# The gate map's one-hot tiles stored token by token, with each slot's values in pairs

## The chip, the cores and the metric

The kernel runs on one core of a Trainium2 chip. The metric is the device time of one execution in microseconds. Engines are named as the profile names them: PE is TensorE (PEld its weight loads), DVE is VectorE, ACT is ScalarE, POOL is GpSimd, SP is the queue of SyncE that issues most transfers.

## The reference

Two transformer blocks over 256 tokens of width 1024. The first is an attention block with a gated feed-forward part. The second has two layers, each a mixing part and then a product-key expert part, `peer`, which is what the change touches:

```python
def peer(h, w_q, sub_keys, u_emb, v_emb):
    ...
    def block(x_t):
        q = jnp.einsum('td,dhk->thk', x_t, w_q).reshape(T, PEER_HEADS, 2, PEER_HALF)
        s = jnp.einsum('thpk,hpnk->thpn', q, sub_keys).astype(jnp.float32)
        sv, si = lax.top_k(s, K)
        cand = (sv[:, :, 0, :, None] + sv[:, :, 1, None, :]).reshape(T, PEER_HEADS, K * K)
        cidx = (si[:, :, 0, :, None] * PEER_NKEYS + si[:, :, 1, None, :]).reshape(T, PEER_HEADS, K * K)
        fv, fpos = lax.top_k(cand, K)
        eidx = jnp.take_along_axis(cidx, fpos, axis=-1)
        gate = jax.nn.softmax(fv, axis=-1)
        u = u_emb[eidx]
        v = v_emb[eidx]
        act = jax.nn.gelu(jnp.einsum('thkd,td->thk', u, x_t).astype(jnp.float32), approximate=False)
        return jnp.einsum('thk,thkd->td', (gate * act).astype(x_t.dtype), v)
```

Every token has 8 heads with 16 experts each, so 128 slots; an expert is a pair (i, j) of two keys, each out of 128, and has a gate.

## The kernel before, in words

The kernel gathers no experts. In each layer it runs over all 16384 of them in two passes. The **first pass** (64 steps, `feat`, lines 298 to 300) computes the activation of every expert for every token. The **second pass** (line 379) sums activation x gate x the expert's row. For the second pass it needs the **gate map** G[i, j, t]: the gate of expert (i, j) for token t, zero where the token didn't choose it.

Float32 accuracy is had from parts. A weight chunk of 128x512 comes from DRAM, ScalarE writes its high part `wh` (line 281), VectorE the low part `wl` as a difference (line 282), and TensorE makes three products of 256 columns for each 128x128 piece (lines 298, 299, 300), so twelve for a chunk and 48 for a step of the first pass. There are five buffers each for `wh` and `wl`.

The gate map is built beside the first pass, as side work in portions. `slots` (lines 1445 to 1447) puts the slots on the partitions: `ijh` holds the two keys of each slot and token, `gth_` and `gtl_` the gate as a high and a low float16 part. `onehots` (lines 1478 to 1480) makes for four tokens, with four DVE operations of 512 float16 elements counting `onelow` (line 1485): `a`, a one at place i of every slot; `e`, a one at place j; `b`, which is `e` times the high gate; and then `e` itself times the low gate. `build` (lines 1491 to 1493) multiplies, for each of the four tokens, `a` with `b` and `a` with `e` on TensorE over the 128 slots, both into one PSUM tile, and ScalarE writes it to G. That is eight products per build, 64 builds in a layer, 128 in the program.

The tiles `a`, `b` and `e` are stored place by place, the four tokens next to each other; one token's 128 values are then four elements apart:

```python
four = [P, P, 4]
return v[:, None, t0:t0 + 4].to_broadcast(four)
nc.vector.tensor_tensor(e, iota4, over(ijh[:, 1], t0), op=OP.is_equal)
nc.tensor.matmul(pg[:, i, :], a[:, :, i], b[:, :, i], start=True, stop=False)
nc.tensor.matmul(pg[:, i, :], a[:, :, i], e[:, :, i], start=False, stop=True)
```

What sets the order: the side work is taken up by costs and a rate (`pace`, `tick`), a portion after each chunk; `onehots` runs two groups ahead of `build`. The program's scheduler then places instructions on each engine, where each engine works strictly in its order. Tiles `a` and `b` share a pool of five buffers with other work; `e` (`ohe`) has three buffers of its own.

Two other products on TensorE read float16 tiles whose 128 values lie next to each other: line 1439, which sorts the slots just ahead of the gate map, and line 266, products for nothing that run where a norm would let TensorE wait (80 at a time).

Of the kernel before, what the change touches and what calls it, by code (L numbers as in the profile page):

```python
# [8 lines left out]
F32 = mybir.dt.float32  # L9
F32R = mybir.dt.float32r  # L10
F16 = mybir.dt.float16
# [3 lines left out]
OP = mybir.AluOpType  # L15
# [4 lines left out]
P = 128  # L20
S = 256
# [12 lines left out]
# the candidate pairs of two descending lists of 16: rows from..to, columns, place of the first  # L34
# [6 lines left out]
# the reciprocal root's first guess, its first step y (C - x y^2) K, and what weighs its second  # L41
# [4 lines left out]
# columns of the per-partition constants, in the order kernel() lays them out  # L46
# [10 lines left out]
NCOL = _n  # L57

# shape-only constants: name -> width of its [128, width] block
# [14 lines left out]
def body(tc, A, out, dbg=None, stop=None):  # L74
# [26 lines left out]
    cols = const.tile([P, NCOL], F32, name="cols")  # L101
    ck = const.tile([P, NCST_KEEP], F32, name="ck")
    nc.scalar.dma_start(ck, A["cst"][:, 0:NCST_KEEP])
    nc.scalar.dma_start(cols, A["cols"])

    def col(name, i=0, n=None):
        a, b = _COL[name]
        return cols[:, a + i:b] if n is None else cols[:, a + i:a + i + n]
# [13 lines left out]
    iota4 = const.tile([P, P, 4], F16, name="iota4")  # L122
    mod = const.tile([P, 2, 48], F32, name="mod")

    def behind(n):
        """what is traced inside gives way to the next n instructions."""
        return tc.high_priority(offset=-n)

    # ------------------------------------------------------------------ helpers
# [11 lines left out]
    def rms_stats(parts, width):  # L141
        """parts: list of [128, width] APs -> [128, len] tile of 1/rms."""
# [10 lines left out]
    def part_sq(ss, src, t, hf, eng):  # L153
        """ss[:, 2t + hf] = the sum of squares of half hf of tile t of src."""
        accum_sq(ss[:, 2 * t + hf:2 * t + hf + 1], src[:, t, hf * 512:(hf + 1) * 512], eng)

    def inv_root(dst, m, v, half, scale):
        """dst = 1/sqrt(m * scale) for scale = 2 ** (-2 half), to float32's accuracy; v: 5 tiles like dst."""
        y, t, p_, h1, h2 = v
        # half the exponent (a division by 2 ** (2 half) is half in it), a step of second order and one of third  # L160
# [14 lines left out]
    def inv_rms(dst, s0, s1, e=D * EPS):  # L175
        """dst [128, 1] = 1/sqrt((s0 + s1 + e) / 1024) (each [128, 1])."""
# [5 lines left out]
    def inv_rms_w(dst, s0, width):  # L182
        """dst [128, 1] = 1/sqrt(s0 / width + EPS)."""
# [5 lines left out]
    def diag(r):  # L189
        """[128, 128] with r [128, 1] on the diagonal: a transpose through it scales its rows."""  # L190
# [4 lines left out]
    def hl_tiles(kc, pl=None, name="hl"):  # L195
        """feature-major operand [128, kc, 256] as exact float32r parts, in pieces of 4 chunks."""
# [13 lines left out]
    def split_psum(hl, k, src, gain=None, bias=None, scale=None):  # L210
        """chunk(s) k of hl from src (PSUM [128, n, 256]); per-partition gain/bias columns."""
# [24 lines left out]
    def to_T(src, kc, hl, gain=None, bias=None, by=None, ks=None):  # L236
        """src(t, k) -> [128 tok, 128] AP; transposed (with rows scaled by the diagonals by[t]), scaled and split into hl."""
# [17 lines left out]
    def follow(i_, name):  # L255
        """the instruction i_ keeps behind the one named, on its own engine."""
        tc.add_manual_dep(i_.ins, name, mybir.DependencyInfo(mybir.DependencyClass.NoSync, mybir.DependencyReason.DATA), reason="order")

    def keep_warm(n):
        """n matrix products for nothing, where a norm lets TensorE wait long enough for its clock to fall."""  # L260
        ps = pmm.tile([P, 512], F32, name="mm")
        name = ada_p["mm"]
        idle = iota4[:, 0:32].rearrange("p j t -> p (j t)")
# [6 lines left out]
    def load_w(dram, off, per, ada=True):  # L270
        """one raw weight tile: [128, per] floats, contiguous by partition."""
# [5 lines left out]
    def split_w(src, n):  # L277
        """float32r parts of src [128, n <= 512]."""
# [16 lines left out]
    def mmT(ps, hl, k, wh, wl, start, stop):  # L295
        """ps [features, 256] += W[k]^T @ chunk k of hl"""
# [5 lines left out]
    # work that runs beside a stream of weights, in portions between its pieces  # L302
# [21 lines left out]
    def feat(hl, dram, off, evac, late=False):  # L324
        """two chunks of 128 features of (h @ W)^T: evac([128, 2, 256]); W as [128 d][2][8 chunks of d][128]."""
# [10 lines left out]
    def proj(hl, kc, dram, off, n, evac, base=0, quiet=0, turn=None):  # L336
        """[256 tok, n <= 512] = hl^T @ W, W at dram[off] as pieces [128, 4 chunks, n]."""
# [9 lines left out]
        for k in order:  # L347
# [3 lines left out]
            while j < m:  # L351
                # the last two chunks tile by tile, so that the first tile's end comes early
# [1420 lines left out]
```

## Time and profile before

| what | value |
|---|---|
| median of three runs | 2292.16 us (2290.6 to 2295.77) |
| the profiled execution: its own time, its span | 2295.77 us, 2295.8 us |
| PE busy | 2259.0 us, 98% |
| DVE busy | 1753.4 us, 76% |
| ACT busy | 1274.5 us, 56% |
| gate map products, lines 1491 and 1492 | 512 each, from 633.3 to 1892.2 us |

The profile is of one execution, the slowest of the three. TensorE's products overlap each other: the duration of one holds its way through the engine, and the distance from one start to the next is what it takes of the engine's time. The stages of the gate map lie at about 633 to 890 us and 1645 to 1892 us.

### The profile page before, as it was taken

To read this page: it belongs to the slowest core of one execution; us is meant where nothing else is said; L and a number is where in the kernel's file an instruction comes from. 1 tells how busy PE (TensorE), PEld (TensorE's weight loads), DVE (VectorE), ACT (ScalarE), POOL (GpSimd) and SP (SyncE) were. 2 spreads that over 40 slices of the span, in tenths; PEclk is the share of its full clock that TensorE was granted. 3 is DMA by queue.
4 is the path that set the end of the run, shared out by engine and by line. 5 is a ranking of instruction groups with operands and counts; after the bars stand their busy time and mean duration, and the time that the engine had idled before them with its cause. 6 is when DMAs were issued, how large, how long until landed. Compare 5 with 4: busy or idle time off the path is not lost.

```text
span 2295.8 us, 40651 instructions
## 1 busy us (share of the span) xinstructions
PE 2259.0 (98%) x15032; PEld 2053.3 (89%) x15032; DVE 1753.4 (76%) x4239; ACT 1274.5 (56%) x2324; POOL 20.6 (1%) x28
## 2 busy tenths in 40 slices
PE   8999999999999999999999999999999999999998
PEld 7889988899999999887778877999999999888886
DVE  7778887798767675688888888896767665777776
ACT  7656555455455555555555565555555555555554
POOL 0000000000000000000000020000000000000000
PEclk9999999999999999999999999999999999999999
DMA  6256786446655555889889533456555557666664
GB/s 249 97 183 249 275 317 236 168 166 234 212 180 175 183 183 185 289 313 322 318 314 325 209 129 134 169 207 222 192 184 174 175 181 248 252 252 237 245 245 145
DMA packets 107161, 503.59 MB, mean 219 GB/s; under 512 B 12369, under 2 KB 13521, under 8 KB 61650
## 3 DMA queue, kind: packets, MB, share of 16 engines
q1 hardware_dynamic: 87954, 465.19, 57.9%
q10 hardware_dynamic: 18720, 33.72, 3.9%
q8 instruction: 117, 1.92, 0.3%
q0 software_dynamic: 288, 2.10, 0.2%
q14 instruction: 82, 0.67, 0.1%
HBM read 464.25 MB, written 36.70 MB: 218 GB/s over the span
## 4 chain that ended last, share of the span: by engine, by line
PE 85%; DVE 7%; DMA 5%; ACT 1%; issue 1%; DVEq 0%; SPq 0%; ACTq 0%
PE acc L379 21%; PE acc L298 14%; PE acc L299 14%; PE acc L300 14%; DMA k<-act 5%; PE acc L287 4%; PE acc L290 3%; PE acc L291 3%; DVE wl L282 3%; PE mm L1491 3%; PE mm L1492 3%; DVE G L436 1%; PE pt L246 1%; PE pt L300 1%; PE pt L299 1%
## 5 line engine op out<-in xcount | busy, mean ns | idle before, releaser
L281 ACT ACTIVATE wh<-w 128x512 fp32r<-128x512 f32 (+1 forms) x1408 | 882.2, 630 | 847.7 <-PE acc L299 383.9
L282 DVE TENSOR_TENSOR wl<-w,wh 128x512 fp32r<-128x512 f32 (+1 forms) x1408 | 954.7, 689 | 283.1 <-ACT wh L281 275.2
L298 PE MATMUL acc<-q,wh 128*128 128x256 f32 x2592 | 745.2, 288 | 0.7 <-ACT q L223 0.7
L299 PE MATMUL acc<-q,wh 128*128 128x256 f32 x2592 | 733.2, 283 | 0.5 <-DVE q L224 0.5
L300 PE MATMUL acc<-q,wl 128*128 128x256 f32 x2592 | 729.8, 283 | 1.2 <-DVE wl L282 1.2
L379 PE MATMUL acc<-wh,q 128*128 128x512 f32 x1984 | 612.1, 390 | 0.0
L298 PEld LDWEIGHTS acc<-q,wh 128*128 128x128 f32 x2592 | 497.9, 192 | 1.5 <-ACT q L223 0.9
L299 PEld LDWEIGHTS acc<-q,wh 128*128 128x128 f32 x2592 | 497.2, 192 | 0.8 <-DVE q L224 0.7
L300 PEld LDWEIGHTS acc<-q,wl 128*128 128x128 f32 x2592 | 495.7, 192 | 1.4 <-DVE wl L282 1.4
L379 PEld LDWEIGHTS acc<-wh,q 128*128 128x128 f32 x1984 | 373.0, 188 | 77.1
L379 PE MATMUL acc<-wl,q 128*128 128x512 f32 x992 | 388.1, 393 | 7.0 <-DVE wl L282 6.7
L379 PEld LDWEIGHTS acc<-wl,q 128*128 128x128 f32 x992 | 186.6, 188 | 52.3 <-DVE wl L282 14.1
L1478 DVE TENSOR_TENSOR ohe<-iota,ijh 128x512 f16<-128x512 f16 x128 | 54.1, 425 | 121.3 <-PE mm L1492 121.3
L1525 DVE SCALAR_TENSOR_TENSOR k<-k,G 128x512 f32<-128x512 f32 x128 | 88.2, 689 | 65.2 <-DMA k<-act 63.8
L1492 PE MATMUL mm<-ohe,k 128*128 128x128 f16 x512 | 128.0, 297 | 0.0
L1491 PE MATMUL mm<-k 128*128 128x128 f16 x512 | 126.6, 293 | 0.0
L1493 ACT ACTIVATE G<-mm 128x512 f32<-128x512 f32 x128 | 76.5, 598 | 38.0 <-PE mm L1492 38.0
L290 PE MATMUL acc<-wl,q 128*128 128x512 f32 (+1 forms) x224 | 89.8, 402 | 0.0
L291 PE MATMUL acc<-wh,q 128*128 128x512 f32 (+1 forms) x224 | 87.1, 397 | 0.0
L1533 DVE TENSOR_TENSOR q<-k,q 128x512 fp32r<-128x512 f32 x126 | 86.2, 684 | 0.7
L287 PE MATMUL acc<-wh,q 128*128 128x512 f32 (+1 forms) x224 | 85.3, 402 | 0.0
L1532 ACT ACTIVATE q<-k 128x512 fp32r<-128x512 f32 x126 | 77.8, 617 | 11.6 <-DVE k L1525 11.4
(458 smaller groups left out, 2316.4 us busy)
## 6 DMA issues: line engine op xcount, KB each, us to landing
w<-in_peer_u_dram SPq DMA_DIRECT2D x128, 1024.0 KB, 5.3
w<-in_peer_v_dram SPq DMA_DIRECT2D x128, 1024.0 KB, 4.9
act<-k ACTq DMA_DIRECT2D x128, 256.0 KB, 4.7
k<-act SPq DMA_DIRECT2D x128, 256.0 KB, 5.3
G<-in_ada_w_dram SPq DMA_DIRECT2D x52, 512.0 KB, 7.3
w<-in_w_gu_dram SPq DMA_DIRECT2D x22, 1024.0 KB, 4.9
adw<-in_ada_w_dram SPq DMA_DIRECT2D x44, 512.0 KB, 5.5
w<-in_peer_w_q_dram SPq DMA_DIRECT2D x16, 1024.0 KB, 4.7
```

Source lines behind the costliest of these rows:

```text
L281: ada_p["act"] = nc.scalar.activation(h[:, :n], src, AF.Copy).ins.name
L282: i_ = nc.vector.tensor_sub(l[:, :n], src, h[:, :n].bitcast(F32))
L287: i_ = nc.tensor.matmul(ps, lh, wh, start=start, stop=False)
L290: nc.tensor.matmul(ps, lh, wl, start=False, stop=False)
L291: i_ = nc.tensor.matmul(ps, ll, wh, start=False, stop=stop)
L298: nc.tensor.matmul(ps, wh, h, start=start, stop=False)
L299: nc.tensor.matmul(ps, wh, l, start=False, stop=False)
L300: nc.tensor.matmul(ps, wl, h, start=False, stop=stop)
L379: nc.tensor.matmul(ps[t, hf], lhs, ww[hf], start=first and lhs is h and ww is wh, stop=last and lhs is l)
L1491: nc.tensor.matmul(pg[:, i, :], a[:, :, i], b[:, :, i], start=True, stop=False)
L1492: nc.tensor.matmul(pg[:, i, :], a[:, :, i], e[:, :, i], start=False, stop=True)
L1525: nc.vector.scalar_tensor_tensor(wt, ag, 1.0 / GATE, G[0][:, 2 * n:2 * n + 2, :], op0=OP.mult, op1=OP.mult)
```

## The change

One token's 128 places now lie in a row, in the order [4 tokens, 128 places]. VectorE must then read one slot's value for 128 places in a row, so every value is stored twice (`ijg`, with a last dimension of 2), and the patterns go by pairs: 4 tokens, 64 times, 2. The four arrays of `slots` become one tile. The iota is no longer written four times over. `e` has two buffers in place of three. Apart from that the per-partition constants `cols` are loaded in two transfers (those of the first block into a pool that is given up later). Comments are dropped, so line numbers move by up to 14.

```diff
-    iota4 = const.tile([P, P, 4], F16, name="iota4")
+    iota = const.tile([P, P], F16, name="iota")
...
-    nc.scalar.dma_start(cols, A["cols"])
+    nc.scalar.dma_start(cols, A["cols"][:, NCOL_1:NCOL])
...
+    cols_1 = xp.tile([P, NCOL_1], F32, name="cols_1")
+    nc.scalar.dma_start(cols_1, A["cols"][:, 0:NCOL_1])
...
-        ijh = ip.tile([P, 2, S], F16, name="ijh")
-        gth_ = ip.tile([P, S], F16, name="gth_")
-        gtl_ = ip.tile([P, S], F16, name="gtl_")
+        ijg = ip.tile([P, 4, S, 2], F16, name="ijg")
...
-            nc.vector.tensor_copy(ijh[:, :, ts_], pt[:, 0:2, :])
-            nc.vector.tensor_copy(gth_[:, ts_], pt[:, 2, :])
-            nc.vector.tensor_sub(gtl_[:, ts_], pt[:, 2, :], gth_[:, ts_])
+            nc.vector.tensor_copy(ijg[:, 0:2, ts_, :], pt[:, 0:2, :].unsqueeze(3).to_broadcast([P, 2, P, 2]))
+            gt = pt[:, 2, :].unsqueeze(2).to_broadcast([P, P, 2])
+            nc.vector.tensor_copy(ijg[:, 2, ts_, :], gt)
+            nc.vector.tensor_sub(ijg[:, 3, ts_, :], gt, ijg[:, 2, ts_, :])
...
-        four = [P, P, 4]
+        four = [P, 4, P // 2, 2]
-        def over(v, t0):
-            return v[:, None, t0:t0 + 4].to_broadcast(four)
+        def over(w, t0):
+            return ijg[:, w, t0:t0 + 4, None, :].to_broadcast(four)
+        def pairs_of(v):
+            return v.rearrange("p t (j a) -> p t j a", a=2)
+        places2 = iota.rearrange("p (j a) -> p j a", a=2)[:, None].to_broadcast(four)
         def onehots(t0):
-            ab = st.tile([P, 2, P, 4], F16, name="k2", bufs=NK2)
+            ab = st.tile([P, 2, 4, P], F16, name="k2", bufs=NK2)
             a, b = ab[:, 0], ab[:, 1]
-            e = ip.tile(four, F16, name="ohe", bufs=3)
-            nc.vector.tensor_tensor(e, iota4, over(ijh[:, 1], t0), op=OP.is_equal)
-            nc.vector.tensor_tensor(a, iota4, over(ijh[:, 0], t0), op=OP.is_equal)
-            nc.vector.tensor_mul(b, e, over(gth_, t0))
+            e = ip.tile([P, 4, P], F16, name="ohe", bufs=2)
+            nc.vector.tensor_tensor(pairs_of(e), places2, over(1, t0), op=OP.is_equal)
+            nc.vector.tensor_tensor(pairs_of(a), places2, over(0, t0), op=OP.is_equal)
+            nc.vector.tensor_mul(pairs_of(b), pairs_of(e), over(2, t0))
...
-            nc.vector.tensor_mul(e, e, over(gtl_, t0))
+            nc.vector.tensor_mul(pairs_of(e), pairs_of(e), over(3, t0))
...
-                nc.tensor.matmul(pg[:, i, :], a[:, :, i], b[:, :, i], start=True, stop=False)
-                nc.tensor.matmul(pg[:, i, :], a[:, :, i], e[:, :, i], start=False, stop=True)
+                nc.tensor.matmul(pg[:, i, :], a[:, i, :], b[:, i, :], start=True, stop=False)
+                nc.tensor.matmul(pg[:, i, :], a[:, i, :], e[:, i, :], start=False, stop=True)
```

The order of instructions moves at two places. The first is VectorE at the head of the first layer's gate map. The numbers tell the tiles apart: `ohe_7902`, `ohe_7946`, `ohe_7984` and `ohe_8039` belong to the first four groups of tokens, `wl_8126` is the low part of a weight chunk. Before:

```order
L1479 TENSOR_TENSOR k2_8038<-iota4_85,ijh_5446 128x512
L1478 TENSOR_TENSOR ohe_8039<-iota4_85,ijh_5446 128x512
L1479 TENSOR_TENSOR k2_8102<-iota4_85,ijh_5446 128x512
L282 TENSOR_TENSOR wl_8126<-w_8122,wh_8125 128x512
L1480 TENSOR_TENSOR k2_8038<-ohe_8039,gth__5447 128x512
L1485 TENSOR_TENSOR ohe_8039<-ohe_8039,gtl__5448 128x512
L282 TENSOR_TENSOR wl_8142<-w_8122,wh_8141 128x512
L1478 TENSOR_TENSOR ohe_8103<-iota4_85,ijh_5446 128x512
```

With the change, at the same place (between the same two splits `wl`):

```order
L1493 TENSOR_TENSOR k2_8038<-iota_85,ijg_5448 128x512
L1492 TENSOR_TENSOR ohe_7984<-iota_85,ijg_5448 128x512
L1493 TENSOR_TENSOR k2_8102<-iota_85,ijg_5448 128x512
L287 TENSOR_TENSOR wl_8126<-w_8122,wh_8125 128x512
L1494 TENSOR_TENSOR k2_7983<-ohe_7984,ijg_5448 128x512
L1499 TENSOR_TENSOR ohe_7984<-ohe_7984,ijg_5448 128x512
L287 TENSOR_TENSOR wl_8142<-w_8122,wh_8141 128x512
L1492 TENSOR_TENSOR ohe_8039<-iota_85,ijg_5448 128x512
```

The one-hot that must wait for a free buffer stands where it stood, but it is the third group's where it was the fourth's: with two buffers the third group is the first to take over a used one, with three it was the fourth. Both take it over from the first group, so both wait for the same build. The two operations behind `wl_8126` move to the third group with it. TensorE's order in the gate map is unchanged.

The second place is ScalarE at the very start, where `q` are the evictions of the transposed input (they need `cols`) and `wh` the high parts of the first weights. Before:

```order
L103 DMA ck<-in_cst_dram 128x128
L104 DMA cols<-in_cols_dram 128x176
L134 ACT_TABLE_LOAD
L134 ACTIVATE k_205,ssx<-x 128x512
L134 ACTIVATE k_219,ssx<-x 128x512
L223 ACTIVATE q_106<-pt,cols 128x256 x3
L281 ACTIVATE wh<-w 128x420 x3
```

With the change:

```order
L105 DMA ck<-in_cst_dram 128x128
L106 DMA cols<-in_cols_dram 128x133
L424 DMA cols_94<-in_cols_dram 128x43
L139 ACT_TABLE_LOAD
L139 ACTIVATE k_207,ssx<-x 128x512
L139 ACTIVATE k_221,ssx<-x 128x512
L286 ACTIVATE wh<-w 128x420 x3
L228 ACTIVATE q_108<-pt,cols_94 128x256 x2
```

The constants come in two transfers, the first block's second, and the three splits now stand ahead of the evictions.

## Rows read from the trace of the kernel before

**Rows 1.** The page's busy time of each engine: us, share of the span, instructions.

```profile
PE 2259.0 (98%) x15032; PEld 2053.3 (89%) x15032; DVE 1753.4 (76%) x4239; ACT 1274.5 (56%) x2324; POOL 20.6 (1%) x28
```

**Rows 2.** The page's chain that ended last, by engine and by line.

```profile
PE 85%; DVE 7%; DMA 5%; ACT 1%; issue 1%; DVEq 0%; SPq 0%; ACTq 0%
PE acc L379 21%; PE acc L298 14%; PE acc L299 14%; PE acc L300 14%; DMA k<-act 5%; PE acc L287 4%; PE acc L290 3%; PE acc L291 3%; DVE wl L282 3%; PE mm L1491 3%; PE mm L1492 3%; DVE G L436 1%; PE pt L246 1%; PE pt L300 1%; PE pt L299 1%
```

**Rows 3.** Windows in both gate-map stages: length; busy us by engine; clock, DMA share, GB/s.

```profile
640.00:880.00 240.00, 240.00 (x2012) 237.26 (x2011) 167.31 (x356) 130.97 (x220) 0.00 (x0) 1.00 0.54 177
1660.00:1900.00 240.00, 240.00 (x2011) 237.33 (x2010) 162.91 (x343) 130.64 (x219) 0.00 (x0) 1.00 0.54 179
```

**Rows 4.** The page's costliest groups, gate-map products: busy us, mean ns, idle before.

```profile
L1492 PE MATMUL mm<-ohe,k 128*128 128x128 f16 x512 | 128.0, 297 | 0.0
L1491 PE MATMUL mm<-k 128*128 128x128 f16 x512 | 126.6, 293 | 0.0
```

**Rows 5.** Timeline of PE around one build: start us, duration us, engine, line, operation.

```profile
705.31 0.28 PE L300 MATMUL acc<-q,wl 128*128 128x256 f32 x1
705.43 0.28 PE L1491 MATMUL mm<-k 128*128 128x128 f16 x1
705.54 0.30 PE L1492 MATMUL mm<-ohe,k 128*128 128x128 f16 x1
...
706.25 0.29 PE L1492 MATMUL mm<-ohe,k 128*128 128x128 f16 x1
706.50 0.28 PE L299 MATMUL acc<-q,wh 128*128 128x256 f32 x1
```

**Rows 6.** Timeline of PE, contiguous float16 products: the warming ones, then line 1439.

```profile
365.42 4.64 PE L266 MATMUL mm<-iota 128*128 128x128 f16 x80
...
602.84 0.28 PE L300 MATMUL acc<-q,wl 128*128 128x256 f32 x1
602.96 0.62 PE L1439 MATMUL mm<-ident_h,tm 128*128 128x128 f16 x8
603.39 0.37 PE L298 MATMUL acc<-q,wh 128*128 128x256 f32 x1
603.60 0.28 PE L299 MATMUL acc<-q,wh 128*128 128x256 f32 x1
```

**Rows 7.** Single lines: ns min/median/max, first and last start.

```profile
L1491 PEld LDWEIGHTS <-k x512: 112/117/120, 633.3 to 1892.0; 128*128 128x128 f16 x171
...
L1439 PEld LDWEIGHTS <-tm x128: 95/98/102, 589.7 to 1616.9; 128*128 128x128 f16 x128
L1439 PE MATMUL mm<-ident_h,tm x128: 218/219/230, 589.8 to 1616.9; 128*128 128x128 f16 x128
```

**Rows 8.** Groups on DVE, 640 to 880 us: busy us, mean ns, idle before, releaser.

```profile
L282 DVE TENSOR_TENSOR wl<-w,wh 128x512 fp32r<-128x512 f32 x130 | 89.4, 688 | 14.1 <-ACT wh L281 14.1
L1485 DVE TENSOR_TENSOR ohe<-ohe,gtl__5448 128x512 f16<-128x512 f16 x57 | 24.1, 423 | 1.4
L1478 DVE TENSOR_TENSOR ohe<-iota,ijh 128x512 f16<-128x512 f16 x56 | 23.8, 425 | 56.4 <-PE mm L1492 56.4
L1479 DVE TENSOR_TENSOR k<-iota,ijh 128x512 f16<-128x512 f16 x57 | 23.8, 418 | 0.1
L1480 DVE TENSOR_TENSOR k<-ohe,gth__5447 128x512 f16<-128x512 f16 x56 | 23.4, 418 | 0.0
```

**Rows 9.** The largest cast of `slots`: ns min/median/max, first and last start.

```profile
L1445 DVE CAST ijh<-mm x4: 417/421/425, 604.2 to 1617.2; 128x256 f16<-128x256 f32 x4
```

**Rows 10.** Timeline of ACT at the start: transfer of constants, evictions, splits.

```profile
1.19 0.45 ACTq L104 DMA_DIRECT2D cols<-in_cols_dram  x1
...
7.12 0.47 ACT L223 ACTIVATE q<-pt,cols 128x256 fp32r<-128x256 f32 x1 [0.24 <-PE pt L244]
...
8.57 1.43 ACT L281 ACTIVATE wh<-w 128x420 fp32r<-128x420 f32 x3
```

**Rows 11.** Timeline of PE at the start: the first products of the first weights.

```profile
9.16 1.07 PE L287 MATMUL acc<-wh,q 128*128 128x420 f32 x2
```

**Rows 12.** Groups of the whole span: a VectorE operation over 1024 float32 elements.

```profile
L436 DVE SCALAR_TENSOR_TENSOR adw<-adw,cact 128x1024 f32<-128x1024 f32 x44 | 53.3, 1219 | 4.3 <-DMA adw<-in_ada_w_dram 2.6 <-ACT cact L430 1.7
```

More of the change, by code (lines that the diff above doesn't have):

```diff
@@ L57 @@
 NCOL = _n
+NCOL_1 = _COL["norm_mix_2"][0]
 _CST = [
@@ L99, in body @@
     pmm = pool("pmm", 2, PSUM)
-    cols = const.tile([P, NCOL], F32, name="cols")
+    cols = const.tile([P, NCOL - NCOL_1], F32, name="cols")
+    first_cols = []
     ck = const.tile([P, NCST_KEEP], F32, name="ck")
     nc.scalar.dma_start(ck, A["cst"][:, 0:NCST_KEEP])
-    nc.scalar.dma_start(cols, A["cols"])
+    nc.scalar.dma_start(cols, A["cols"][:, NCOL_1:NCOL])
     def col(name, i=0, n=None):
         a, b = _COL[name]
-        return cols[:, a + i:b] if n is None else cols[:, a + i:a + i + n]
+        c = first_cols[0] if a < NCOL_1 else cols
+        if a >= NCOL_1:
+            a, b = a - NCOL_1, b - NCOL_1
+        return c[:, a + i:b] if n is None else c[:, a + i:a + i + n]
     def cst(name):
@@ L262, in keep_warm @@
         name = ada_p["mm"]
-        idle = iota4[:, 0:32].rearrange("p j t -> p (j t)")
+        idle = iota
         for _ in range(n):
@@ L417, in body @@
     x = xp.tile([P, 2, D], F32, name="x")
+    cols_1 = xp.tile([P, NCOL_1], F32, name="cols_1")
+    nc.scalar.dma_start(cols_1, A["cols"][:, 0:NCOL_1])
+    first_cols.append(cols_1)
     ada_q.extend((l, n) for l in range(2) for n in range(48))
@@ L602, in body @@
     nc.sync.dma_start(io_[:, 0:P], A["cst"][:, _CO["iota"][0]:_CO["iota"][1]])
-    nc.vector.tensor_copy(iota4, io_[:, 0:P].unsqueeze(2).to_broadcast([P, P, 4]))
+    nc.vector.tensor_copy(iota, io_[:, 0:P])
     tri = cst_tile(ap_, "tri")
```

## The prediction

> **What bounds the kernel now.** I read the page first: busy shares and the chain that ended last, then the stage that the change touches, then single products in it. TensorE is busy in 98% of the span [rows 1], and 85% of the chain lies on it [rows 2]. The two lines of the gate map, L1491 and L1492, hold about 3% of the span each on that chain [rows 2], so they are work that sets the end, not work beside it. Their stage shows why: between 640 and 880 us, and again between 1660 and 1900 us, TensorE is busy for all 240 of 240 us at the full granted clock, VectorE for 167 and 163, ScalarE for 131, and the DMA engines for 0.54 [rows 3]. TensorE waits for nothing there. Whatever leaves its stream in this stage leaves the end, as long as VectorE keeps ahead.
>
> A busy TensorE says nothing on how fast its products are, because they overlap: one product of L1491 lasts 293 ns and one of L1492 297 ns [rows 4], yet they start about 0.12 us apart [rows 5]. So I price by start to start. In rows 5 a build (eight products, four tokens with a high and a low part) begins at 705.43; the second product of the chunk behind it begins at 706.50. That is 1.07 us for eight builds and one 256-column product, and such a product takes 0.12 us of the stream (602.84 to 602.96 in rows 6). Eight strided builds cost 0.95 us, 0.118 us each, with no extra step into the next chunk.
>
> **The change, part by part.** *The operands in one run.* Each product now reads 128 neighbouring float16 values of a token where it read every fourth, on both operands; number and size of the products stay. The trace has such products already. L1439 sorts the slots with 128x128 float16 products from contiguous tiles, in the same stream between the same chunks: eight begin at 602.96 and the second product of the chunk behind them begins at 603.60, so 0.64 us for what takes 1.07 us with strided operands [rows 6]. The products that keep TensorE warm read one contiguous float16 tile: 80 of them last 4.64 us against 0.62 us for the eight, (4.64 - 0.62) / 72 = 0.056 us apiece [rows 6]. Of the 0.64 us, 8 x 0.056 = 0.45 are the products, 0.12 the chunk's own one, and 0.07 a step into the chunk that the strided builds hide.
>
> A build thus saves 1.07 - 0.64 = 0.43 us. There are 256 / 4 = 64 builds in each of two layers, 128 in all, which agrees with 512 products on each of the two lines, four a build [rows 4]: 128 x 0.43 = **55 us**. Bounds: if the step into the chunk vanishes, 8 x (0.118 - 0.056) = 0.50 us a build, 64 us in all; if the weight loads set the pace at their own 98 ns (L1439's, against 117 for L1491 [rows 7]), 8 x (0.118 - 0.098) = 0.16 us, 20 us in all. I take 0.43: L1439 has the same shapes, type and neighbours, and loads a new weight tile for every product too.
>
> [...]
>
> *The one-hots on VectorE.* Four operations of 512 float16 elements per group of four tokens stay four, at 418 to 425 ns [rows 8]. Their patterns change: the slot's value was read as runs of four, and is now read as one pair, 64 times over per token. No row shows runs of two. The near end is 0.42 us, the same operation with runs of four; the far one is 0.69 us, which is what 512 float32 elements of L282 take [rows 8]. I take 0.42: the result is still float16 with neighbours side by side, and the repeated operand was repeated before too. The cover: a group lasts 240 / 56.5 = 4.25 us now and would last 3.82 us, and VectorE is busy for 167 / 56.5 = 2.96 of it, 78% then. 56 of its idle microseconds are waits at L1478 for the build that frees a buffer [rows 8]; these shrink.
>
> *Two one-hot buffers in place of three.* The order shows that the place of L1478 between the splits `wl` does not move; only the group that it makes is one later build away. It waits for the same build as before. The multiplication by the low part, which its build needs, follows after 0.42 + 0.42 + 0.69 + 0.42 + 0.42 = 2.4 us of VectorE's work; two builds and four chunks of 1.44 us later, over 6 us, that build is due. I put it at nought: the work that hides it is those four chunks. With that cover gone, a build would stand for up to the 2.4 us, and VectorE's splits of the next chunk would be late next.
>
> *Paired lists.* The casts in `slots` write twice the elements: the largest takes 421 ns for 256 elements [rows 9], becomes at most 0.69 us for 512, and the two others are half its size. Four times three such steps of at most 0.27 us are 3 us of VectorE's time in all, from 604 us on and again 1000 us later, beside TensorE's stream. I put them at nought; uncovered they would cost those 3 us. The iota is cast once and becomes shorter. Nought.
>
> *The constants in two transfers.* At the start ScalarE issues one transfer more (0.45 us for the present one) and takes three splits `wh`, 1.43 us, ahead of the first evictions `q`, which come first now at 7.12 us [rows 10]. The first product, at 9.16 us, needs both [rows 11]. So it moves by between nothing and the 1.4 us; I take 0.5 us.
>
> **Sum.** 55.0 - 0.5 = 54.5 us off. The profiled execution took 2295.8 us, its span; 2295.8 - 54.5 = 2241.3. It is the slowest of three, 3.6 us above their median of 2292.16, so on the median's scale **2237.7 us**, say 2238. Its own range is 2228 to 2252: the vanished step at one end, at the other four fifths of the gain and the whole price at the start.
>
> **Rivals.**
>
> *Pairs run at one element per cycle.* If the four operations take 0.69 us, VectorE needs 2.96 + 4 x 0.27 = 4.04 us per group, more than TensorE's 3.82. It becomes the bound, and at best 4.25 - 4.04 = 0.21 us x 128 = 27 us are won: 2265 to 2292, middle 2278. For it: no row shows such runs. Against: the runs of four did not slow down.
>
> *Pairs cost so much that VectorE loses time (the other side).* [...] It decides from (4.25 - 2.96) / 4 = 0.32 us more per operation, 0.74 us [rows 8, 12]. Any price beyond that makes the kernel slower than before. Nothing in the trace points to it.
>
> *The step between elements was not what cost.* Then 0.118 us belongs to these products, contiguous or not, and the time is 2292.2 + 0.5 = 2293. Rows 6 speak against it, unless alternating two moving tiles over one weight tile costs something that L1439 doesn't pay. [...]
>
> *Weight loads at 98 ns set the pace:* 20 us won, 2273.
>
> **How the numbers follow.** Forecast 0.80; one element per cycle 0.06; weight loads 0.04; step not the cost 0.05; slower through the pairs 0.05. The predicted time is the forecast's. The range is 2227 to 2262: the forecast's bounds, stretched at the upper end towards the rivals that still win; the four rivals, 0.20, lie beyond it. A measurement of this kernel tells about 0.2%, 4.6 us, from no change. Faster by more: 0.80 + 0.04 + 0.06 = 0.90; the same 0.05; slower 0.05.
>
> **What would show it.** Right: products of the gate map lasting about 219 ns like L1439's [rows 7], starting 0.056 us apart, 0.64 us from a build's first product to the second of the next chunk; TensorE still busy for all of the stage, which is 27 us shorter in each layer; the four operations at 0.42 us; shorter waits of VectorE at the first one-hot; no change elsewhere. Wrong: the four operations near 0.69 us with TensorE waiting for `wl`; or products that still start 0.1 us apart or more.

## The result and the profile after

The changed kernel takes **2235.8 us** (median of four runs, 2233.88 to 2238.66) against 2292.4 us for the kernel before beside it (2290.6 to 2295.77): the ratio is 0.9754, 95% interval 0.974 to 0.9768. That is 56.6 us less. The forecast was 2238, 54.5 us less, with a range of 2227 to 2262. On another chip, where the kernel before took 2297.61 us, the same program took 2242.67 us (0.9762, 0.9745 to 0.9778).

The profiled execution took 2235.14 us, with a span of 2233.4. The page's busy times answer [rows 1]:

```profile
PE 2201.5 (99%) x15032; PEld 1997.3 (89%) x15032; DVE 1754.2 (79%) x4239; ACT 1265.4 (57%) x2324; POOL 21.5 (1%) x28
```

TensorE ran as many instructions as before and was busy for 57.5 us less; VectorE did the same 1754 us of work in a shorter span. The page's chain of work that ended last, by engine and by line, answers [rows 2]:

```profile
PE 86%; DVE 6%; DMA 5%; ACT 1%; issue 1%; SPq 0%; DVEq 0%; ACTq 0%
PE acc L384 23%; PE acc L303 15%; PE acc L304 14%; PE acc L305 14%; DMA k<-act 4%; PE acc L292 4%; PE acc L295 4%; PE acc L296 4%; DVE wl L287 3%; PE mm L1505 1%; PE mm L1506 1%; PE pt L251 1%; DVE G L444 1%; PE pt L305 1%; PE pt L304 1%
```

The gate map's two lines are now L1505 and L1506, 1% each where they had 3% each. The chunk products of the first pass are L303 to L305, the eviction of a build L1507, the one-hots L1492 to L1494 and the multiplication by the low part L1499. The page's costliest groups (busy us, mean ns, idle before) answer [rows 4]:

```profile
L1505 PE MATMUL mm<-k 128*128 128x128 f16 x512 | 72.3, 222 | 0.0
L1506 PE MATMUL mm<-ohe,k 128*128 128x128 f16 x512 | 70.7, 219 | 0.0
```

One line's instructions (ns min/median/max) answer [rows 7]. Load and product have become those of the slot sort, 98 and 219 ns:

```profile
L1505 PEld LDWEIGHTS <-k x512: 96/98/100, 635.3 to 1830.6; 128*128 128x128 f16 x171
L1505 PE MATMUL mm<-k x512: 219/219/230, 635.3 to 1830.7; 128*128 128x128 f16 x171
```

How much a build takes is read from PE's timeline around one of them (start us, duration us), as in [rows 5]:

```profile
706.70 0.28 PE L305 MATMUL acc<-q,wl 128*128 128x256 f32 x1
706.83 0.23 PE L1505 MATMUL mm<-k 128*128 128x128 f16 x1
706.89 0.22 PE L1506 MATMUL mm<-ohe,k 128*128 128x128 f16 x1
...
707.23 0.22 PE L1506 MATMUL mm<-ohe,k 128*128 128x128 f16 x1
707.25 0.36 PE L303 MATMUL acc<-q,wh 128*128 128x256 f32 x1
707.46 0.28 PE L304 MATMUL acc<-q,wh 128*128 128x256 f32 x1
```

From the build's first product, 706.83, to the second one of the chunk behind it, 707.46, it is 0.63 us where it was 1.07. Over all builds that stand alone the median is 0.632 us (122 of 128; before 1.064 over 124). The products start 56 ns apart (before 118). The gate map's products run from 635 to 873 us and from 1593 to 1831; before they ran from 633 to 898 and from 1627 to 1892 (ahead of the prediction they are given as 633 to 890 and 1645 to 1892). Each layer's stage is 27 us shorter.

The windows inside both stages (length; busy us of PE, PEld, DVE, ACT, POOL; clock, DMA share, GB/s) answer [rows 3]:

```profile
640.00:860.00 220.00, 220.00 (x2055) 217.51 (x2054) 170.91 (x363) 129.32 (x223) 0.00 (x0) 1.00 0.59 199
1620.00:1840.00 220.00, 220.00 (x2049) 217.59 (x2047) 166.76 (x351) 129.68 (x224) 0.00 (x0) 1.00 0.60 198
```

TensorE is still busy for all of the stretch at the full granted clock. VectorE's share rose from 70 to 78%, and has room left. Its groups from 640 to 860 us (busy us, mean ns, idle before) answer [rows 8]:

```profile
L287 DVE TENSOR_TENSOR wl<-w,wh 128x512 fp32r<-128x512 f32 x133 | 91.6, 688 | 15.5 <-ACT wh L286 15.3
L1499 DVE TENSOR_TENSOR ohe<-ohe,ijg 128x512 f16<-128x512 f16 x58 | 24.6, 424 | 1.5
L1494 DVE TENSOR_TENSOR k<-ohe,ijg 128x512 f16<-128x512 f16 x58 | 24.3, 419 | 0.0
L1492 DVE TENSOR_TENSOR ohe<-iota,ijg 128x512 f16<-128x512 f16 x57 | 24.3, 426 | 30.5 <-PE mm L1506 30.5
L1493 DVE TENSOR_TENSOR k<-iota,ijg 128x512 f16<-128x512 f16 x57 | 23.0, 420 | 1.2 <-DMA act<-k 1.1
```

The four operations on pairs take 419 to 426 ns, as the runs of four did. The wait for the build that frees a buffer (at L1492) shrank from 56.4 us in 240 to 30.5 in 220.

**Where the 62.4 us between the two profiled executions lie.** I add up by TensorE's marks. From the first chunk product behind the last scores of the keys (the 33rd chunk product of the first pass over the experts) to the first product of the second pass, the trace holds the whole gate map and the same 3040 chunk products before and after. This stretch is called the first pass from here on: 429.7 and 429.8 us became 402.0 and 402.0, so 27.7 + 27.8 = **55.5 us**. The second pass of the first layer fell from 358.6 to 352.4 us, 6.2 us, but it isn't the change's: its length is 359.2 in the repeat of the changed kernel, while the second layer's is 344.3 in both kernels and in the repeat. The stretch between the layers, from the end of that pass to the second layer's first pass, is 2.5 us shorter (205.8 and 203.3 us). There the granted clock of the kernel before is 0.50 in the windows from 1313 to 1316 and from 1412 to 1415 us, and that of the changed kernel 1.00 all through. Over the runs with the same idle products the stretch takes 202.9 to 203.3 us in the six traces whose clock stays at 1.00 in it and 204.3 to 206.3 in the five whose clock falls. Two of those five have the new moving layout, so it doesn't keep the clock from falling; whether it makes that rarer, some 1 to 3 us a run, is open. Ahead of the first pass 2.0 us were lost, 0.6 of them by the first idle products. Of the rest, the windows from 418 us on show a part (columns as above):

```profile
418.00:420.00 2.00, 2.00 (x7) 1.57 (x8) 0.89 (x3) 0.69 (x2) 0.00 (x0) 0.65 0.00 0
420.00:422.00 2.00, 2.00 (x7) 1.41 (x5) 0.63 (x2) 0.09 (x1) 0.00 (x0) 0.50 0.00 0
```

The granted clock falls to 0.50 after 2 us (416 to 418) in which TensorE ran 11 products; the mark behind it is 1.4 us further back than the one before it. In the same windows of the kernel before and of the changed kernel's repeat it stands at 1.00, with 10 to 12 products in each, so this too is not the change's. So the change is worth 55.5 us in the first passes, less what the start costs, and apart from what it may do to the clock between the layers.

### The profile page after: what moved, and what is told of

The parts are those of the page before. It is cut to its first block, busy times and chain, and to the rows that moved or that the text cites. A ratio compares the mean times of both kernels' runs of the same rounds, so it can differ in the third digit from the quotient of the medians.

```text
span 2233.4 us, 40655 instructions
## 1 busy us (share of the span) xinstructions
PE 2201.5 (99%) x15032; PEld 1997.3 (89%) x15032; DVE 1754.2 (79%) x4239; ACT 1265.4 (57%) x2324; POOL 21.5 (1%) x28
## 4 chain that ended last, share of the span: by engine, by line
PE 86%; DVE 6%; DMA 5%; ACT 1%; issue 1%; SPq 0%; DVEq 0%; ACTq 0%
PE acc L384 23%; PE acc L303 15%; PE acc L304 14%; PE acc L305 14%; DMA k<-act 4%; PE acc L292 4%; PE acc L295 4%; PE acc L296 4%; DVE wl L287 3%; PE mm L1505 1%; PE mm L1506 1%; PE pt L251 1%; DVE G L444 1%; PE pt L305 1%; PE pt L304 1%
## 5 line engine op out<-in xcount | busy, mean ns | idle before, releaser
L286 ACT ACTIVATE wh<-w 128x512 fp32r<-128x512 f32 (+1 forms) x1408 | 881.3, 630 | 827.9 <-PE acc L304 335.5
L303 PE MATMUL acc<-q,wh 128*128 128x256 f32 x2592 | 744.7, 288 | 0.7 <-ACT q L228 0.7
L305 PE MATMUL acc<-q,wl 128*128 128x256 f32 x2592 | 730.0, 283 | 0.0
L303 PEld LDWEIGHTS acc<-q,wh 128*128 128x128 f32 x2592 | 495.3, 191 | 1.3 <-ACT q L228 0.9
L305 PEld LDWEIGHTS acc<-q,wl 128*128 128x128 f32 x2592 | 495.1, 191 | 0.0
L1492 DVE TENSOR_TENSOR ohe<-iota,ijg 128x512 f16<-128x512 f16 x128 | 54.2, 425 | 63.7 <-PE mm L1506 63.6
L1507 ACT ACTIVATE G<-mm 128x512 f32<-128x512 f32 x128 | 75.7, 593 | 1.9 <-PE mm L1506 1.9
L1505 PE MATMUL mm<-k 128*128 128x128 f16 x512 | 72.3, 222 | 0.0
L1506 PE MATMUL mm<-ohe,k 128*128 128x128 f16 x512 | 70.7, 219 | 0.0
```

Source lines behind the costliest of these rows:

```text
L286: ada_p["act"] = nc.scalar.activation(h[:, :n], src, AF.Copy).ins.name
L303: nc.tensor.matmul(ps, wh, h, start=start, stop=False)
L305: nc.tensor.matmul(ps, wl, h, start=False, stop=stop)
L1505: nc.tensor.matmul(pg[:, i, :], a[:, i, :], b[:, i, :], start=True, stop=False)
L1506: nc.tensor.matmul(pg[:, i, :], a[:, i, :], e[:, i, :], start=False, stop=True)
```

## The experiments

**The theories.** Of a product's two operands one, the weights, has a load of its own in the trace (LDWEIGHTS on PEld, 15032 of them beside 15032 products), and the other is called the moving operand; a step is the distance in memory from one of an operand's 128 values to the next. T1: the step of the moving operand is what cost 62 ns a product, and a step in the weight load is hidden beside the products. T2: the weight load's step cost it. T3: either of them is enough. The rival to all three is that another part of the change (two buffers, the constants' two transfers) brought some of the gain. The first four runs share one chip, on which the kernel before took 2298.52 us, 6 more than on the first one, so I go by ratios and by the first passes in the traces; the times that were expected of them are on the first chip's scale.

### One operand strided at a time

The changed kernel with the weights' one-hot interleaved by four tokens again:

```diff
+        def by4(v):
+            return v.rearrange("p t j -> p (t j)").rearrange("p (j t) -> p j t", t=4)
...
-            nc.vector.tensor_tensor(pairs_of(a), places2, over(0, t0), op=OP.is_equal)
+            nc.vector.tensor_tensor(pairs_of(by4(a).rearrange("p j t -> p t j")), places2, over(0, t0), op=OP.is_equal)
...
-                nc.tensor.matmul(pg[:, i, :], a[:, i, :], b[:, i, :], start=True, stop=False)
+                nc.tensor.matmul(pg[:, i, :], by4(a)[:, :, i], b[:, i, :], start=True, stop=False)
...
```

> The changed kernel, but the one-hot of the first list (the operand that is loaded as weights) lies as before, four tokens in turn, so that the weight load reads with a step of 8 bytes; both moving operands stay contiguous. T1 (the step of the moving operand costs all of the 62 ns a product, the loads' step is hidden beside the products): products start 0.056 us apart, and the time is that of the changed kernel, 2234 to 2239 us. T2 (the step of the weight load costs it): 0.118 us apart, 2290 to 2295 us. T3 (either step is enough): also 2290 to 2295 us here.

Measured: 2244.76 us, ratio 0.9758 (0.9732 to 0.9784), as far below the kernel before as the changed kernel. PE's timeline around a build:

```profile
705.66 0.25 PE L1508 MATMUL mm<-k 128*128 128x128 f16 x1
705.74 0.22 PE L1509 MATMUL mm<-ohe,k 128*128 128x128 f16 x1
...
706.31 0.28 PE L304 MATMUL acc<-q,wh 128*128 128x256 f32 x1
```

0.65 us where the contiguous weights give 0.63. First passes of 403.3 and 402.8 us, 1 us over the changed kernel's each. The price turned up where I had not looked for one, on VectorE's groups from 640 to 860 us:

```profile
L1496 DVE TENSOR_TENSOR k<-iota,ijg 128x512 f16<-128x512 f16 x57 | 74.1, 1342 | 0.9 <-DMA act<-k 0.9
L1495 DVE TENSOR_TENSOR ohe<-iota,ijg 128x512 f16<-128x512 f16 x59 | 25.5, 432 | 7.1 <-PE mm L1509 7.1
```

Writing the one-hot with a step of 8 bytes takes 1342 ns where its neighbours take 0.42 us. VectorE's operations overlap too: from its start to the next one's, where they follow each other at once, the strided one takes 1.12 us and its neighbours 0.34. It stayed hidden: the wait at the first one-hot fell from 30.5 to 7.1 us, the one for ScalarE at `wl` from 15.3 to 1.1, and TensorE was busy for all of the 220.

The other half, with both moving operands strided and the slots' values for them in runs of four:

```diff
-            nc.vector.tensor_tensor(pairs_of(e), places2, over(1, t0), op=OP.is_equal)
+            nc.vector.tensor_tensor(by4(e), iota4, over4(jgl[:, 0], t0), op=OP.is_equal)
...
-                nc.tensor.matmul(pg[:, i, :], a[:, i, :], b[:, i, :], start=True, stop=False)
+                nc.tensor.matmul(pg[:, i, :], a[:, i, :], by4(b)[:, :, i], start=True, stop=False)
...
```

> The other half: the weights contiguous, the two moving operands with their step of 8 bytes as before. T1: products 0.118 us apart, no gain is left, 2290 to 2295 us. T2: 0.056 us apart, 2234 to 2239 us. T3: 2290 to 2295 us. If both this run and the one with strided weights come out at 2236, only both steps together cost; if both lie between, each has a part.

Measured: 2295.69 us, ratio 0.9987 (0.9975 to 1.0). PE's timeline around a build:

```profile
706.62 0.27 PE L1515 MATMUL mm<-k 128*128 128x128 f16 x1
706.71 0.30 PE L1516 MATMUL mm<-ohe,k 128*128 128x128 f16 x1
...
707.66 0.28 PE L305 MATMUL acc<-q,wh 128*128 128x256 f32 x1
```

1.04 us, against 1.07 with both strided; first passes of 428.9 us, 0.9 under the kernel before's. T1 holds; T2 and T3 are out. Of the 0.432 us that a build gained, the weights' step has 0.014 to 0.018 and the moving operand's the rest.

### A step of two values

```diff
-        four = [P, 4, P // 2, 2]
+        four = [P, 2, P, 2]
...
-                nc.tensor.matmul(pg[:, i, :], a[:, i, :], b[:, i, :], start=True, stop=False)
+                nc.tensor.matmul(pg[:, i, :], pairs_of(a)[:, i // 2, :, i % 2], pairs_of(b)[:, i // 2, :, i % 2], start=True, stop=False)
...
```

> The changed kernel with tokens interleaved in twos: both operands of every product step by 4 bytes, and the slots' values are read in runs of two tokens, not stored in pairs. [...] If the price is a threshold at anything but neighbours, 0.118 us and 2290 to 2295 us. If it grows with the step, in between: about 0.08 us, 512 x 2 x 0.02 = 20 us over the changed kernel, 2256 us.

Measured: 2244.21 us, ratio 0.9759 (0.973 to 0.9789). PE's timeline around a build:

```profile
709.81 0.23 PE L1504 MATMUL mm<-k 128*128 128x128 f16 x1
709.88 0.22 PE L1505 MATMUL mm<-ohe,k 128*128 128x128 f16 x1
...
710.46 0.28 PE L304 MATMUL acc<-q,wh 128*128 128x256 f32 x1
```

0.65 us a build, the products 58 ns apart, first passes of 402.85 us. So a step of 4 bytes costs 2 ns a product, and 8 bytes cost 60. "Anything but neighbours" is out as the rule, and so is a price that grows evenly from the first step on. Also, VectorE needs no stored pairs here: runs of two tokens, read side by side, take 419 to 425 ns as well.

### All of the change but the layout

```diff
-            e = ip.tile(four, F16, name="ohe", bufs=3)
+            e = ip.tile(four, F16, name="ohe", bufs=2)
...
-    nc.scalar.dma_start(cols, A["cols"])
+    nc.scalar.dma_start(cols, A["cols"][:, NCOL_1:NCOL])
...
```

> The kernel before with all of the change but the layout: two one-hot buffers in place of three, and the constants in two transfers. By my sum: two buffers nought, the start 0 to 1.4 us later (0.5 taken, and 1.1 us seen at the first product of the changed kernel): 2292 to 2294 us. The rival, that part of the 56 us is not the layout's: 2289 us or less. If two buffers cost something while builds are long: over 2296 us, with TensorE waiting at the builds.

Measured: 2299.73 us, ratio 1.0 (0.9987 to 1.0013). Builds of 1.064 us as before, first passes of 429.8 and 430.2 us. The wait at the first one-hot is what it was with three buffers:

```profile
L1486 DVE TENSOR_TENSOR ohe<-iota,ijh 128x512 f16<-128x512 f16 x56 | 23.8, 426 | 56.5 <-PE mm L1500 56.5
```

The time is over the 2296 us that would have spoken for a cost of two buffers, but so is the kernel before beside it, at 2298.52. To within 3 us (the interval), none of the gain is here, and none of it is lost here.

### Steps by themselves

The kernel before; each group of 80 idle products becomes eight kinds of ten. Their results are thrown away in both kernels. (The prediction and the expectation call them products that keep TensorE warm; what they do for the granted clock, no run here shows.)

```diff
+        s3 = flat[:, 0:3 * P].rearrange("p (j t) -> p j t", t=3)[:, :, 0]
+        s4 = iota4[:, :, 0]
...
+                yield lambda: nc.tensor.matmul(ps[:, 0:P], s1, s3, start=True, stop=True)
...
+                yield lambda: nc.tensor.matmul(ps[:, 0:P], s4, s1, start=True, stop=True)
...
-                i_ = nc.tensor.matmul(ps[:, 0:P], idle, idle, start=True, stop=True)
+                i_ = make()
```

> The kernel before; only its idle products that keep TensorE warm differ: each group of 80 becomes eight kinds of ten 128x128 float16 products, with the steps of (weights, moving operand) in bytes (2, 2), (2, 4), (2, 6), (2, 8), (2, 16 within each half of the columns), (4, 2), (8, 2) and (8, 8). From the runs so far: (2, 2) and (4, 2) at 0.056 us from start to start, (2, 4) at 0.056 to 0.060, (2, 8) and (8, 8) at 0.116 to 0.118, (8, 2) at 0.056 to 0.060. Where is the edge? [...] Threshold between 4 and 8: (2, 6) is either 0.056 or 0.116. Price in proportion to the bytes that are spanned, from 4 bytes on: (2, 6) at 0.087 and (2, 16) at 0.23 us; price per product that is the same for every wide step: (2, 16) at 0.116 us too.

Measured: 2302.85 us in a single run, so only its trace is used. PE's timeline of the first group (start us, duration us of the ten):

```profile
365.65 0.73 PE L272 MATMUL mm<-iota 128*128 128x128 f16 x10
366.22 0.74 PE L274 MATMUL mm<-iota 128*128 128x128 f16 x10
366.80 1.04 PE L276 MATMUL mm<-iota 128*128 128x128 f16 x10
367.68 1.33 PE L278 MATMUL mm<-iota 128*128 128x128 f16 x10
368.82 2.45 PE L280 MATMUL mm<-iota 128*128 128x128 f16 x10
371.09 0.74 PE L282 MATMUL mm<-iota 128*128 128x128 f16 x10
371.67 0.72 PE L284 MATMUL mm<-iota 128*128 128x128 f16 x10
372.23 1.34 PE L286 MATMUL mm<-iota 128*128 128x128 f16 x10
373.39 0.52 PE L246 MATMUL pt<-dg,xf 128*128 128x128 f32 x3
```

A tenth of the distance between two starts is one product's price:

| line | weights' step, bytes | moving step, bytes | us per product |
|---|---|---|---|
| L272 | 2 | 2 | 0.057 |
| L274 | 2 | 4 | 0.058 |
| L276 | 2 | 6 | 0.088 |
| L278 | 2 | 8 | 0.114 |
| L280 | 2 | 16 | 0.227 |
| L282 | 4 | 2 | 0.058 |
| L284 | 8 | 2 | 0.056 |
| L286 | 8 | 8 | 0.116 |

The price follows the bytes that the moving operand spans, from 4 bytes a column on: 128 x 4 / 58, 128 x 6 / 88, 128 x 8 / 114 and 128 x 16 / 227 are 8.8, 8.7, 9.0 and 9.0 bytes per ns and partition. (With 16 bytes the two halves of the columns lie within the same 1024 bytes, so it is the step from column to column that counts, not how much memory is touched.) The third group of idle products, from 1309.59 us on, gives 0.058, 0.088, 0.115 and 0.227 us for these steps. Neighbouring float16 values need only 4.5 bytes per ns (128 x 2 / 57). The weights' step is free here, to within 2 ns. Of the three forms in the expectation, the one in proportion to the span, which gave 0.087 us at 6 bytes and 0.23 at 16, is right.

### The slots' values not in pairs

```diff
-        ijg = ip.tile([P, 4, S, 2], F16, name="ijg")
+        ijg = ip.tile([P, 4, S], F16, name="ijg")
...
-            return ijg[:, w, t0:t0 + 4, None, :].to_broadcast(four)
+            return ijg[:, w, t0:t0 + 4, None].to_broadcast(four)
...
```

> The changed kernel with the slots' values not stored in pairs: the four one-hot operations read one float16 value again and again, 128 times, in place of a pair 64 times. [...] By the nearest row, 0.69 us an operation, VectorE would need 0.69 + 4 x 0.69 = 3.4 us and what else it does in a group, 4.0 us, against TensorE's 3.72 us: VectorE becomes the bound and the time is about 0.3 x 128 = 40 us over the changed kernel at most, 2250 to 2280 us. If the single value is as good as the pair, 0.42 us and the changed kernel's time, 2234 to 2245 us (on this chip the kernel before took 2298.5).

Measured: 2259.35 us, ratio 0.9835 (0.982 to 0.985), about 0.8 points, 18 us, behind the changed kernel. One of the four operations and the stretch from 640 us on (columns as above):

```profile
L1492 DVE TENSOR_TENSOR k<-iota,ijg 128x512 f16<-128x512 f16 x52 | 35.4, 690 | 6.9 <-DMA act<-k 6.9
```

```profile
640.00:860.00 220.00, 218.63 (x1991) 214.20 (x1989) 206.78 (x339) 125.11 (x214) 0.00 (x0) 1.00 0.57 195
```

All four take 689 to 691 ns. VectorE is busy for 94% of the window and TensorE no longer for all of it. First passes are 409.0 and 411.7 us, 7.0 and 9.7 over 402.0. It is less than the 40 us that the expectation gave as the most: the map is spread over more chunks and ends 28 us later (901.8 in place of 873.3), in a stretch of 42 us in which the changed kernel had chunks alone. The edit also moved TensorE's order: 57 of the 64 builds in each layer stand as one product and seven, with chunk products between them. Such a build and two chunk products take 0.239 + 0.577 us in place of 0.632 + 0.12, 0.064 us more, or 3.6 us a layer. What TensorE waits for in the rest is told by its waits from 632 to 920 us (first line) and from 1607 to 1897 (us in total, times, longest):

```profile
PE acc L303 <- ACT k L1555: 2.7, 4, 0.7
PE acc L303 <- ACT k L1555: 3.5, 5, 1.0
PE mm L1504 <- DVE k L1493: 1.2, 2, 1.1
```

Only 1.2 us are waits for VectorE itself; L1555 is ScalarE's eviction of the activations. So an operation has the price of the rival that put it at 0.69 us, and the pairs, at 0.42, keep that away, but the loss came mostly by the order and by waits for ScalarE. What the rate alone would cost with TensorE's order kept, no run shows.

### Two builds side by side

```diff
-        for t0 in range(0, S + 8, 4):
+        for t0 in range(0, S + 4, 4):
+            if t0 >= 8 and t0 % 8 == 0:
+                add(0.0, build, t0 - 8)
+                add(0.0, build, t0 - 4)
...
-            if 4 <= t0 < S + 4:
-                add(0.35, onelow, t0 - 4)
-            if t0 >= 8:
-                add(0.0, build, t0 - 8)
+                add(0.35, onelow, t0)
```

> The changed kernel with two builds side by side (16 products between chunks in place of 8, half as many stretches), and each low part multiplied right behind its one-hots. In the changed kernel a build and the first product of the chunk behind take 0.632 us, two adjacent builds with theirs 1.079 us; a chunk's own product takes 0.12 us, so a pair of builds saves 2 x 0.632 - 1.079 - 0.12 = 0.065 us, 64 times: 4.2 us, 0.9981 of the changed kernel's time. The rival: with two buffers the one-hots of both builds are made only after the builds before, the builds come late, TensorE waits, and the time is the same or longer.

Measured: 2240.61 us, ratio 0.9748 (0.9734 to 0.9761), not to be told from the changed kernel's 0.9754. The trace shows first passes of 400.9 us, 1.1 us less each in place of 2.1: of the pairs only 40 stood as 16 products (1.079 us as expected), the others fell apart, most of them into 9 and 7.

For the last three runs the layout in twos, which stores no pairs and so leaves room, took back the third one-hot buffer and the constants' single transfer, without and with builds in pairs; the changed kernel ran beside them.

> The changed kernel once more, on the chip of the two runs beside it, so that they can be set against it: ratio to the kernel before 0.974 to 0.977, the whole first pass over the experts 402.0 us in each layer (before 429.8), whatever the chip; what differs between chips lies in the second pass of the first layer (352 to 365 us so far, where the second layer's takes 344).

Measured: 2242.67 us, ratio 0.9762 (0.9745 to 0.9778), first passes of 402.0 us twice, and a second pass of 359.2 us in the first layer. The first passes are the same to 0.01 us on another chip.

```diff
-            e = ip.tile([P, 4, P], F16, name="ohe", bufs=2)
+            e = ip.tile([P, 4, P], F16, name="ohe", bufs=3)
...
-    nc.scalar.dma_start(cols, A["cols"][:, NCOL_1:NCOL])
+    nc.scalar.dma_start(cols, A["cols"])
```

> The run with tokens in twos, which stores no pairs and so has the room, with three one-hot buffers again and the constants in one transfer, as in the kernel before. By my terms: buffers nought, the start 0 to 1 us earlier, the step of 4 bytes 0.019 us a build as seen, so first passes of 402.85 us as with two buffers and one transfer less, and a time within 2 us of it and of the changed kernel. If two buffers held something back, the first passes are shorter than 402.8 us.

Measured: 2246.24 us, ratio 0.977 (0.9756 to 0.9783). First passes of 402.8 us: a third buffer brings nothing. (With stored pairs a third buffer was not tried.) The time is 3.6 us over the changed kernel's beside it, where 2 were allowed, but the two intervals overlap: 1.6 us are in the first passes, and the second pass of the first layer, 361.3 us, is 2.0 longer in the profiled execution. PE's timeline shows the first weights' product where [rows 11] had it:

```profile
9.10 0.72 PE L288 MATMUL acc<-wh,q 128*128 128x420 f32 x1
```

With two transfers it stands at 10.1 to 10.3 us in seven kernels. By the first idle products the difference is gone: 366.3 us here, 365.0 to 367.2 in those.

```diff
+        def twobuilds(t0):
+            build(t0)
+            build(t0 + 4)
...
+            if t0 >= 8 and t0 % 8 == 0:
+                add(0.0, twobuilds, t0 - 8)
```

> The same with two builds always side by side, which the third buffer lets stand as 16 products throughout (with two buffers some split into 9 and 7, and the first passes gave 1.1 us each in place of 2.1). 16 products with the 4-byte step and the chunk's first behind them take 1.119 us, two times eight 2 x 0.651: with the chunk's own 0.12 us a pair saves 2 x 0.651 - 1.119 - 0.12 = 0.063 us, 32 pairs a layer: first passes of 402.85 - 2.0 = 400.8 us, 2.3 us in all under the changed kernel, 0.1% and at the edge of what can be measured. The rival: VectorE's one-hots come late for the pairs and the first passes are no shorter than 402.8 us.

Measured: 2238.09 us, ratio 0.9738 (0.9723 to 0.9752). All 64 pairs stand as 16 products, 1.118 us each, and the first passes take 401.1 us: 1.7 less than with eight, where 2.0 were expected, 0.9 less than the changed kernel's. It is the lowest ratio of the study, but its interval meets that of the changed kernel beside it. No version was shown to beat the change.

## Why the prediction was right

**The operands in one run, 55 us: right, and for the reason given.** The step from 1.07 to 0.64 us a build was read from the slot sort's products. Measured: 1.064 to 0.632, the same 0.43. The two layers gained 55.5 us in the first passes. The step into the chunk that I had taken along (0.07 us) is there too: two adjacent builds take 1.079 us and two single ones 1.264, which at 0.12 for the chunk's product leaves 0.065 for each step saved. Neither bound was reached. What the trace of before couldn't show, and the runs with one operand strided do, is that the price lies on the moving side, all but 0.02 us a build.

**The weight loads.** They fell from 117 to 98 ns and set no pace: products start every 56 ns. The rival at 2273 us took the duration of a load for its spacing, and loads overlap as products do (PEld's timeline has three of 0.10 us starting at 706.84, 706.89 and 706.95). With strided weights alone the time stayed, at a ratio of 0.9758.

**The one-hots, 0.42 us an operation: right.** 419 to 426 ns [rows 8]. The far end, 0.69, was a real price, but of another form: a single value read 128 times costs 690 ns. Pairs stay at 0.42 us, and so do runs of two tokens (419 to 425 ns, in the run with a step of two values); the single value doesn't.

**Two buffers, nought: right.** Undone on either side, nothing moved: 56.4 and 56.5 us of waiting with the old layout, first passes of 402.85 and 402.8 us with tokens in twos. VectorE's share of 78% came as forecast. TensorE's order, given ahead of the prediction as unchanged, does move at one place: the last build of each layer stands as one product and seven with three chunk products between them. The old layout with two buffers has it too, the three buffers with tokens in twos don't, and it costs 0.06 us.

**The paired lists, nought: right.** Three operations of 421, 280 and 286 ns became 688, 415 and 418. Four times 0.53 us are 2.1 us of VectorE's time, where at most 3 were allowed, and TensorE's first passes show no trace of them.

**The start, 0.5 us: the size is open, the sign at the first product right.** ScalarE's timeline answers [rows 10], and PE's [rows 11]:

```profile
1.67 0.45 ACTq L424 DMA_DIRECT2D cols<-in_cols_dram  x1
...
8.40 1.44 ACT L286 ACTIVATE wh<-w 128x420 fp32r<-128x420 f32 x3 [1.52 <-DMA w<-in_w_in_dram]
9.75 0.82 ACT L228 ACTIVATE q<-pt,cols 128x256 fp32r<-128x256 f32 x2
```

```profile
10.25 0.72 PE L292 MATMUL acc<-wh,q 128*128 128x420 f32 x1 [0.46 <-ACT q L228]
```

The three splits do stand ahead of the evictions now, the second transfer of the constants is issued, and the first product begins 1.1 us later. What of that reaches the end is less than what executions differ by: 0.6 us at the first idle products here, nothing that can be seen in the runs side by side.

**The rivals.** The step not being the cost is out by the two runs with one operand strided. Pairs at 0.69 us an operation are out at 0.42 us. (Among the chances this rival is called one element per cycle; no run shows VectorE's cycle, and 0.69 us is what the 512 float32 elements of L282 take, 688 ns [rows 8].) Brought about by the single value, that price gave 18 us of loss, where my rival had left 27 us of the 55 at best, a loss of 28: it didn't count that the map can run on into the 42 us of chunks behind it, as it did, nor that TensorE's order would move. The rival that was slower than before had no ground: a step in what VectorE writes did reach 1342 ns, beyond the 0.74 us from which it should decide, but for one operation of the four, and the waits for the build and for ScalarE covered it.

**The rest.** One bound doesn't come out of its terms: four fifths of the gain with the whole price at the start give 2292.2 - 44 + 1.4 = 2249.6 us, where the forecast's own range says 2252. Nothing hangs on it. 54.5 us were forecast, 56.6 measured between medians that each rest on four runs spread over 5 us; the 2 us between them are not explained further, since the second pass of the first layer alone moves by more (352 to 365 us) from one execution to another.

## What to carry to other kernels

Price overlapped products by start to start, and look in the same stream for products of the same shape with another layout: here eight of them gave the gain to within 1 us. Lay the moving operand of a 128x128 float16 product so that its columns lie at most 4 bytes apart: 0.058 us a product here, against 0.057 for neighbours and 0.088 at 6 bytes. The weights may step, by up to 8 bytes as tried here (0.056 us by themselves, 2 ns a product more in a build), but the VectorE operation that wrote them with a step of 8 bytes took 1342 ns where those beside it took 419 to 435. When a broadcast operand has to become innermost, store or read it as pairs: here that kept an operation on 512 float16 elements at 0.42 us, where a single value took 0.69.

## What the runs showed of the hardware that was not expected

**A wide moving operand doesn't feel the lower clock.** In the second group of idle products of the run with steps by themselves, the granted clock fell after TensorE had run its wide-step kinds: it is 1.00 from 450 to 451 us, 0.83 in the next and 0.50 from 452 to 455. The timeline of PE there, and the windows inside the same kinds in the first group and the second (columns as above):

```profile
452.21 1.27 PE L284 MATMUL mm<-iota 128*128 128x128 f16 x10
453.28 1.36 PE L286 MATMUL mm<-iota 128*128 128x128 f16 x10
454.46 0.71 PE L246 MATMUL pt<-dg,xf 128*128 128x128 f32 x2
```

```profile
371.67:372.30 0.63, 0.63 (x14) 0.63 (x12) 0.63 (x8) 0.00 (x0) 0.00 (x0) 1.00 0.98 397
372.30:373.50 1.20, 1.20 (x13) 1.18 (x11) 0.14 (x2) 0.00 (x0) 0.00 (x0) 1.00 0.93 372
452.30:453.20 0.90, 0.90 (x12) 0.90 (x10) 0.00 (x0) 0.00 (x0) 0.00 (x0) 0.50 0.97 410
453.30:454.50 1.20, 1.20 (x13) 1.20 (x11) 0.00 (x0) 0.00 (x0) 0.00 (x0) 0.50 0.79 335
```

At 0.50 the products with a contiguous moving operand (L284) take (453.28 - 452.21) / 10 = 0.107 us in place of 0.056, and those with a step of 8 bytes (L286) (454.46 - 453.28) / 10 = 0.118 in place of 0.116. For the same two kinds the third group gives (1317.02 - 1315.96) / 10 = 0.106 and (1318.22 - 1317.02) / 10 = 0.120 us. So it isn't TensorE's granted clock that limits the wide ones. That their bytes come at some 9 a ns and partition at either clock fits the proportion to the span; that the coming of the bytes is the limit is argued, and which part of the chip would set that rate, no run here tells.

**A step of 8 bytes on VectorE's output** makes an operation on 512 float16 elements last 1342 ns in place of 419; from start to start it is 1.12 us in place of 0.34, 0.8 us more. On TensorE's side of the same tile, as weights, it costs 2 ns a product (0.014 to 0.018 us a build of eight).
